# Moving the weights' sums to ScalarE's DMA queue, and a second tile for the last multiplications, in a hybrid encoder layer on one core

## Chip, core and metric

The kernel runs on one core of a Trainium2 chip. The metric is the device time of one execution in microseconds (us); several executions were timed, and one more was taken with the hardware profiler. A core has five engines that matter here: TensorE (PE, matrix products; PEld is its weight load), VectorE (DVE), ScalarE (ACT), GpSimd (POOL) and SyncE (SP, which here only issues DMAs). Each engine works through its own instructions in order; DMAs are issued as instructions of an engine, here of SP, GpSimd or ScalarE, and wait in that engine's order.

## The reference

One layer of an encoder over 512 tokens of width 1024: four parallel token mixers with one input projection, merged by gates; a cross-attention into 256 memory tokens; and a gated feed-forward part. All is float32. The change touches the feed-forward part only:

```
hf  = _rms_norm(x, norm_ffn_pre[l])
u   = _dwconv_causal(hf @ w_up[l], ffn_dw[l]) + ffn_dw_b[l]       # w_up: 1024 x 5632, three taps along the tokens
u_g, u_v = jnp.split(u, 2, axis=-1)
yff = (jax.nn.silu(u_g) * u_v) @ w_down[l]                        # w_down: 2816 x 1024
x   = x + _rms_norm(yff, norm_ffn_post[l])                        # mean square over the 1024 columns, then a weight per column
```

## The kernel before

A float32 product is made of three products of a coarser type: each operand is split into a high part (a cast on ScalarE, L183 or L1384) and the rest, its low part (a subtraction on VectorE, L184 or L1385), and `mm3` (L232) issues high x high, high x low and low x high. Weights come by DMA from SP's queue into tiles `wr` (two of them), are split into tiles `wh` and `wl` (four of each, taken in turn), and are then read by PE. `run_blocks` (L196) splits a block's weights three blocks ahead of its products.

**The up-projection** (`up_jobs`, L1285). 44 blocks n of 128 columns of w_up, gate and value columns in turn, n = 2j + i. After the first four blocks each takes 24 products of 128 x 512 on PE into one PSUM bank; the banks have two tags, `mm` and `av`, in turn, with two banks each. `done` (L1288) empties the bank: ScalarE adds the bias and the last tap (L1292), VectorE the two other taps (L519, called in L1293) into the same tile `c`. After a value block ScalarE takes a tanh (L1296) and VectorE forms silu(gate) x value (L1297, L1299) into the tiles `qa` and `qb`.

**The sums for the down-projection.** The product with w_down is made by a scheme with seven products of 2 x 2 blocks in place of eight (M1 to M7), which needs sums and differences of blocks on both sides. `activation_sums` (L1341) forms those of the activations on GpSimd, four instructions for each of 11 pairs. Those of the weights are formed during the up-projection: `weight_pair(q)` (L1348) loads the pair q of 128 x 1024 blocks of w_down into two tiles `wp` (two pairs fit, as the tag has four buffers), and `weight_sums(q)` (L1353) makes four subtractions or additions in place on VectorE (L1357 to L1360) and stores both tiles to `sums`, a buffer in DRAM (L1362). Before the change the loads and the stores are DMAs of GpSimd's queue. The first two pairs are loaded when block 3 is done; the sums of pair q, its stores and the load of pair q + 2 are placed at block n = 3q + 6, the sums right behind the taps of that block.

**The down-projection** (`down_jobs`, L1364). 22 steps load tiles `dw` from w_down and from `sums` on SP's queue (L1379); `dw` has the same four buffers as `wp`. Phase 0 computes M1, M6, M5 and M7 for all 11 pairs, phase 1 M2, M3 and M4. `middle` (L1446) joins the first four; the last four pairs of phase 1 are held back and done product by product in `ends` (L1490), whose instructions on PE, VectorE, ScalarE and GpSimd keep the order that is written there: M4 for token tiles 0 and 1, then M2 and M3 of tile 0, then M2 and M3 of tile 1. For each, `whole` (L1494) adds the product to a partial sum on VectorE (L1502), `result` (L1469) takes the mean square on ScalarE (`square`, L1439, an activation that also reads out its sum) and multiplies by the post norm's weight on VectorE (L1478); when both halves of a token tile are there, GpSimd makes the reciprocal root (`rstd_of`, L262 and L265), and `finish` (L1481) scales, adds the residual (L1487) and stores (L1488, SP's queue). `finish` of a tile is written after the next product's `result`. The last half is scaled and stored in two pieces.

The lines of the code that order the sums before the change:

```
q = n // 3 - 2
if n % 3 == 0 and q < NF // 2:
    with tc.issue_after(st["last"]):
        weight_sums(q)
    if q + 2 < NF // 2:
        weight_pair(q + 2)
```

Of the kernel before, what the change touches and what calls it, by code (L numbers as in the profile page):

```python
# [16 lines left out]
F32 = mybir.dt.float32  # L17
F32R = mybir.dt.float32r
AF = mybir.ActivationFunctionType
# [5 lines left out]
P = 128  # L25
S = 512
D = 1024
# [6 lines left out]
NF = DFF // P  # L34
EPS = 1e-6
WB = 2 * 520
# [46 lines left out]
def hybrid_layer(ctx: ExitStack, tc: tile.TileContext, a: dict, out: bass.AP):  # L83
    nc = tc.nc
    V, A, G, PE, SP = nc.vector, nc.scalar, nc.gpsimd, nc.tensor, nc.sync


    gp = ctx.enter_context(tc.tile_pool(name="g", bufs=1))
# [7 lines left out]
    def bank(tag=None):  # L96
        if tag is None:
            turn_of.n += 1
            tag = "av" if turn_of.shared and turn_of.n % 2 else "mm"
        return psum.tile([P, 512], F32, tag=tag, name=f"ps_{tag}", bufs=2)  # L100
# [7 lines left out]
    w_up, w_down = a["w_up"][0], a["w_down"][0]  # L108
# [19 lines left out]
    for i in range(8):  # L128
        n = ("wh", "wl")[i % 2]
# [3 lines left out]
        elif i < 6:  # L133
            n = ("fz_raw", "fz", "fe", "fu", "fd")[i - 1]
# [55 lines left out]
    def cols(w, c0, n=P, k0=0, nk=NK):  # L190

        return w[k0 * P:(k0 + nk) * P, c0:c0 + n].rearrange("(k p) c -> p k c", p=P), [P, nk, n]
# [45 lines left out]
    def channel_major(ps, w, act, sl=slice(0, S)):  # L238

        hi, lo = w  # L240
        nk = hi.shape[1]
        for k in range(nk):
            mm3(ps[:, sl], hi[:, k, :], lo[:, k, :], act[0][:, k, sl], act[1][:, k, sl], k == 0, k == nk - 1)
            if k == 3 < nk - 1:
                bg.tick()
# [51 lines left out]
    m1 = tc.tile_pool(name="m1", bufs=1)  # L297
# [62 lines left out]
    for i, plan in enumerate(plans):  # L360
        r_t = m1p.tile([P, P], F32, tag="fbias" if i == 2 else "ck", name=f"rows{i}", bufs=2)
        n = 0
# [116 lines left out]
    def pc(name, j=0, n=1):  # L479
        i, base = where[name]  # L480
        return par[i][:, base + j:base + j + n]
# [33 lines left out]
    def taps(dst, src, w, n):  # L515

        for k in range(n - 1):
            s = n - 1 - k
            ins = V.scalar_tensor_tensor(dst[:, s:], src[:, :S - s], w(k), dst[:, s:], ALU.mult, ALU.add)  # L519
        return ins  # L520
# [486 lines left out]
    ns = SimpleNamespace()  # L1007
# [262 lines left out]
    sums = dram.tile([NF // 2 * P, 2 * D], F32, name="sums")  # L1270
    ns.pair = {}

    def open_ffn():
        bg.drain("n1")
        close(ns.work_)
        close(ns.xp_)
        close(ns.xm_)
        ns.fp_, ns.fp = new_pool("ffn", False)
        ns.work = ns.fp
        ns.quart = [(ns.fp.tile([P, 4, S // 2], F32, tag=f"qa{q}", name="qa"),  # L1280
                     ns.fp.tile([P, 3, S // 2], F32, tag=f"qb{q}", name="qb")) for q in range(NF // 2)]
        ns.post = ns.fp.tile([P, D], F32, name="g_ffn")
        G.dma_start(ns.post, a["norm_ffn_post"][0].partition_broadcast(P))

    def up_jobs():  # L1285
        st, held = {}, []

        def done(j, i, ps):  # L1288
            if i == 0:
                st[j] = ns.fp.tile([P, 2, S], F32, tag="c", name="c", bufs=2)  # L1290
            c, ch = st[j], i * NF + j
            A.activation(c[:, i], ps, AF.Identity, bias=pc("fb", ch), scale=pc("fdw2", ch))  # L1292
            st["last"] = taps(c[:, i], ps, lambda k: pc("fdw01", k * 44 + ch), 3).ins  # L1293
            if i == 1:
                th = ns.fp.tile([P, S], F32, tag="th", name="th")
                A.activation(th, c[:, 0], AF.Tanh, scale=0.5)  # L1296
                V.scalar_tensor_tensor(th, th, 1.0, c[:, 0], ALU.add, ALU.mult)  # L1297
                x = ns.quart[j // 2]
                V.scalar_tensor_tensor(x[j % 2][:, 0:2].rearrange("p a b -> p (a b)"), th, 0.5, c[:, 1],  # L1299
                                       ALU.mult, ALU.mult)  # L1300
                if j % 2:
                    activation_sums(*x)


        for n in range(2 * NF):
            def body(hi, lo, n=n):
                j, i = divmod(n, 2)
                if n > 3:
                    ps = bank()
                    channel_major(ps, (hi, lo), ns.hf)  # L1310
                    done(j, i, ps)
                    q = n // 3 - 2
                    if n % 3 == 0 and q < NF // 2:
                        with tc.issue_after(st["last"]):
                            weight_sums(q)
                        if q + 2 < NF // 2:
                            weight_pair(q + 2)
                    return
                if n == 0:
                    bg.drain("n0")  # L1320
                ps = bank(("mm", "sc")[n % 2])
                (channel_major if n else by_pass)(ps, (hi, lo), ns.hf, slice(0, S // 2))
                held.append((j, i, ps, (hi, lo)))
                if n == 3:
                    open_ffn()
                    for j, i, ps, w in held:
                        (channel_major if i or j else by_pass)(ps, w, ns.hf, slice(S // 2, S))
                        done(j, i, ps)
                    weight_pair(0)
                    weight_pair(1)  # L1330
            yield *cols(w_up, n % 2 * DFF + n // 2 * P), body, V, same, HALF_SHIFT if n < 4 else 0
# [9 lines left out]
    def activation_sums(x, z):  # L1341

        G.tensor_tensor(x[:, 2], x[:, 1], z[:, 1], ALU.add)
        G.tensor_tensor(x[:, 3], x[:, 0], x[:, 1], ALU.subtract)
        G.tensor_tensor(x[:, 1], x[:, 2], x[:, 0], ALU.subtract)
        G.tensor_tensor(z[:, 2], z[:, 0], x[:, 1], ALU.subtract)

    def weight_pair(q):  # L1348
        pair = ns.pair[q] = [ns.fp.tile([P, D], F32, tag="dw", name="wp", bufs=4) for _ in range(2)]
        for i in range(2):  # L1350
            G.dma_start(pair[i], w_down[(2 * q + i) * P:(2 * q + i + 1) * P, :])

    def weight_sums(q):  # L1353

        pair = ns.pair.pop(q)
        (b11, b12), (b21, b22) = ((x[:, :S], x[:, S:]) for x in pair)
        V.tensor_tensor(b22, b22, b12, ALU.subtract)  # L1357
        V.tensor_tensor(b12, b12, b11, ALU.subtract)
        V.tensor_tensor(b11, b22, b11, ALU.add)
        V.tensor_tensor(b21, b21, b11, ALU.subtract)  # L1360
        for i in range(2):
            G.dma_start(sums[q * P:(q + 1) * P, i * D:(i + 1) * D], pair[i])  # L1362

    def down_jobs():  # L1364
        pairs, hold, half = NF // 2, 4, S
# [77 lines left out]
        gains = [slice(i * 512, (i + 1) * 512) for i in range(2)]  # L1443
# [25 lines left out]
        def result(t, i, x, dst, pieces=1):  # L1469

            ms[t, i] = square(x, i, pieces)
            r = None
            if (t, 1 - i) in ms:
                *early, last = ms[t, 1 - i] + ms[t, i]
                if len(early) == 2:
                    G.tensor_tensor(early[0], early[0], early[1], ALU.add)
                r = rstd_of(ns.fp, [early[0], last])
            V.tensor_tensor(dst, x, ns.post[:, gains[i]], ALU.mult)  # L1478
            return r
# [10 lines left out]
        def ends():  # L1490

            m1, u, z7, z = (parts[n] for n in ("m1", "u", "z7", "z"))

            def whole(name, t, x, pieces=1):  # L1494

                for c in range(pieces):
                    cut = slice(c * S // pieces, (c + 1) * S // pieces)
                    for q, job, ws in held:
                        for (n, a), w in zip(work[1, job], ws):
                            if n == name:  # L1500
                                step(name, t, q, a, w, 1, cut)
                    V.tensor_tensor(x[:, cut], x[:, cut], banks[name][t][:, cut], ALU.add)  # L1502
                return x

            waiting = None
            with tc.manual_schedule(engines={e.engine for e in (PE, V, A, G)}):
                for name, t, i, x in (("M4", 0, 0, z7), ("M4", 1, 0, z7), ("M2", 0, 0, m1), ("M3", 0, 1, u),
                                      ("M2", 1, 0, m1), ("M3", 1, 1, u)):
                    token = t + 2 * (name == "M4")
                    x = whole(name, t, x[:, t])  # L1510
                    r = result(token, i, x, x)
                    if waiting:
                        finish(*waiting)
                        waiting = None
                    if r is not None:
                        waiting = token, {1: z[:, t], 0: x} if name == "M4" else {0: m1[:, t], 1: x}, r
                finish(*waiting)

        def body(phase, q, job, ws):
# [67 lines left out]
```

## Time and profile before

| | us |
|---|---|
| median of 3 runs (lowest to highest) | 1073.1 (1071.56 to 1074.53) |
| profiled execution | 1070.76 |
| its span, first to last instruction | 1069.0 |
| PE busy in the span | 1056.0 |
| DVE / ACT / POOL busy in the span | 764.4 / 489.2 / 171.1 |
| mean granted TensorE clock | 0.996 |

In a row of a timeline stand the start and the length in us, the engine, the line, the operation, what it writes and reads (names of tiles, with the buffer numbers left out) with shapes, how many instructions are merged (x), and in brackets how long the engine had been idle and what released it. POOLq, ACTq and SPq are the issuing of DMAs and the like; such instructions are not counted as busy. Ends of products on PE are modelled. The up-projection's steady part runs from about 735 to 942 us of the span and the down-projection from there; the last product ends near 1057.6 us.

### The profile page before, as it was taken

To read this page: it belongs to the slowest core of one execution; us is meant where nothing else is said; L and a number is where in the kernel's file an instruction comes from. 1 tells how busy PE (TensorE), PEld (TensorE's weight loads), DVE (VectorE), ACT (ScalarE), POOL (GpSimd) and SP (SyncE) were. 2 spreads that over 40 slices of the span, in tenths; PEclk is the share of its full clock that TensorE was granted. 3 is DMA by queue.
4 is the path that set the end of the run, shared out by engine and by line. 5 is a ranking of instruction groups with operands and counts; after the bars stand their busy time and mean duration, and the time that the engine had idled before them with its cause. 6 is when DMAs were issued, how large, how long until landed. Compare 5 with 4: busy or idle time off the path is not lost.

```text
span 1069.0 us, 14449 instructions
## 1 busy us (share of the span) xinstructions
PE 1056.0 (99%) x5387; PEld 898.2 (84%) x5387; DVE 764.4 (72%) x1211; ACT 489.2 (46%) x809; POOL 171.1 (16%) x277
## 2 busy tenths in 40 slices
PE   9999999999999999999999999999999999999995
PEld 8888888888888988888888899998888888888884
DVE  7899996467666367766464386787778888777795
ACT  5322222466564365555453364554333333446661
POOL 4000001000101024323000030031223332111002
PEclk9999999999999999999999999999999999999998
DMA  6433333332222243332354443235576766626652
GB/s 212 112 98 90 93 100 98 99 90 75 74 80 81 59 126 95 97 99 81 97 158 149 146 139 99 80 87 190 177 246 217 225 221 219 211 79 205 210 186 79
DMA packets 158524, 141.04 MB, mean 132 GB/s; under 512 B 5056, under 2 KB 134701, under 8 KB 158454
## 3 DMA queue, kind: packets, MB, share of 16 engines
q1 hardware_dynamic: 149555, 108.50, 33.8%
q0 software_dynamic: 8896, 31.61, 8.7%
q8 instruction: 42, 0.69, 0.3%
q14 instruction: 29, 0.23, 0.1%
q10 hardware_dynamic: 2, 0.00, 0.0%
HBM read 126.45 MB, written 13.65 MB: 131 GB/s over the span
## 4 chain that ended last, share of the span: by engine, by line
PE 98%; DVE 1%; ACT 0%; issue 0%; POOL 0%; POOLq 0%; DVEq 0%; ACTq 0%
PE ps_mm L225 52%; PE ps_av L225 30%; PE ps_sc L225 8%; PE ps_tr L229 3%; PE ps_tr L225 2%; PE ps_mm L432 1%; PE ps_av L432 1%; PE ps_mm L374 0%; ACT junk L1439 0%; DVE o L1487 0%; PE ps_sc L379 0%; DVE wr L1487 0%; DVE wr L1478 0%; DVE z L1487 0%; DVE o L1502 0%; DVE wr L1502 0%
## 5 line engine op out<-in xcount | busy, mean ns | idle before, releaser
L183 ACT CAST wh<-wr 128x1024 fp32r<-128x1024 f32 (+1 forms) x150 | 157.0, 1050 | 291.6 <-PE ps_mm L225 183.9
L184 DVE TENSOR_TENSOR wl<-wr,wh 128x1024 fp32r<-128x1024 f32 (+1 forms) x150 | 189.2, 1263 | 113.1 <-ACT wh L183 112.7
L225 PE MATMUL ps_mm<-hth,wh 128*128 128x512 f32 (+1 forms) x616 | 231.4, 382 | 0.3 <-ACT hth L152 0.2
L225 PE MATMUL ps_mm<-hth,wl 128*128 128x512 f32 (+1 forms) x616 | 230.0, 380 | 0.0
L225 PE MATMUL ps_mm<-htl,wh 128*128 128x512 f32 (+1 forms) x616 | 229.9, 380 | 0.0
L225 PEld LDWEIGHTS ps_mm<-hth,wh 128*128 128x128 f32 x616 | 114.3, 188 | 21.2 <-ACT hth L152 0.5
L225 PEld LDWEIGHTS ps_mm<-hth,wl 128*128 128x128 f32 x616 | 114.0, 188 | 21.0
L225 PEld LDWEIGHTS ps_mm<-htl,wh 128*128 128x128 f32 x616 | 114.0, 188 | 20.5 <-DVE htl L153 0.2
L225 PE MATMUL ps_av<-hth,wh 128*128 128x512 f32 (+1 forms) x328 | 122.4, 373 | 0.0
L225 PE MATMUL ps_av<-htl,wh 128*128 128x512 f32 (+1 forms) x328 | 122.4, 373 | 0.0
L225 PE MATMUL ps_av<-hth,wl 128*128 128x512 f32 (+1 forms) x328 | 122.3, 373 | 0.0
L586 DVE SCALAR_TENSOR_TENSOR y<-y,par,y 128x499 f32<-128x499 f32 (+28 forms) x120 | 82.4, 731 | 0.2
L225 PEld LDWEIGHTS ps_av<-htl,wh 128*128 128x128 f32 x328 | 61.7, 188 | 10.9
L225 PEld LDWEIGHTS ps_av<-hth,wh 128*128 128x128 f32 x328 | 61.6, 188 | 10.9
L225 PEld LDWEIGHTS ps_av<-hth,wl 128*128 128x128 f32 x328 | 61.5, 188 | 10.8
L225 PE MATMUL ps_mm<-y,wh 128*128 128x512 f32 x192 | 61.2, 394 | 0.0
L1385 DVE TENSOR_TENSOR wl<-dw,wh 128x1024 fp32r<-128x1024 f32 x32 | 40.2, 1261 | 12.3 <-ACT wh L1384 12.2
L1384 ACT CAST wh<-dw 128x1024 fp32r<-128x1024 f32 x32 | 33.4, 1051 | 23.0 <-PE ps_tr L225 8.4
L225 PEld LDWEIGHTS ps_mm<-y,wh 128*128 128x128 f32 x192 | 35.4, 188 | 6.8
L909 POOL TENSOR_SCALAR fbias<-ck,cq 128x128 f32<-128x128 f32 (+3 forms) x32 | 27.5, 865 | 68.1 <-DVE st L915 63.9
L225 PE MATMUL ps_mm<-y,wl 128*128 128x512 f32 x96 | 37.6, 392 | 0.0
L1296 ACT ACTIVATE th<-c 128x512 f32<-128x512 f32 x22 | 13.9, 632 | 49.4 <-DVE c L519 49.4
(436 smaller groups left out, 2026.4 us busy)
## 6 DMA issues: line engine op xcount, KB each, us to landing
wr<-in_w_up SPq DMA_DIRECT2D x44, 512.0 KB
wr<-in_w_in SPq DMA_DIRECT2D x38, 512.0 KB
wr<-in_w_gate SPq DMA_DIRECT2D x32, 512.0 KB
wp<-in_w_down POOLq DMA_DIRECT2D x22, 512.0 KB, 5.5
sums<-wp POOLq DMA_DIRECT2D x22, 512.0 KB, 4.2
dw<-sums SPq DMA_DIRECT2D x44, 256.0 KB
wr<-in_w_branch SPq DMA_DIRECT2D x16, 512.0 KB
dw<-in_w_down SPq DMA_DIRECT2D x11, 512.0 KB
```

Of the source, the lines that this page charges most:

```text
L183: order(A.copy(hi, raw[:, :n]))
L184: low.tensor_tensor(lo, raw[:, :n], hi.bitcast(F32), ALU.subtract)
L225: PE.matmul(ps, lhs, rhs, start=start, stop=stop)
L229: PE.transpose(ps, x, ident[:n, :n])
L432: keep(PE.matmul(banks[c][:, :S // 2], w[p == 1][:, k, c * P:(c + 1) * P], ht[p == 2][:, i * 4 + k, :S // 2], start=(i, p, k) == (0, 0, 0) ...
L586: V.scalar_tensor_tensor(dst[:, s:], src[:, :S - s], pc("conv_dw", k * 4 + j), dst[:, s:], ALU.mult, ALU.add)
L909: G.tensor_scalar(bias[:, :w], ck[j][:, :w], -1.0, cq[:, qt, head:head + 1], ALU.mult, ALU.add)
L1296: A.activation(th, c[:, 0], AF.Tanh, scale=0.5)
L1384: A.copy(hi, x)
L1385: V.tensor_tensor(lo, x, hi.bitcast(F32), ALU.subtract)
```

## The change

Part one splits the storing from the sums and moves loads and stores of the pairs to ScalarE's queue. The four sums stay at block n = 3q + 6 behind its taps; the two stores are placed at the next block behind its bias activation (L1292), and the load of pair q + 2 one block later, again behind that activation. Part two gives the multiplications by the post norm's weight in `ends` a destination of their own: two tiles of the tag `dw` and one of the tag `wr`, which are free by then. The sum that the square reads is no longer overwritten; `finish` reads the new tiles.

```diff
-            A.activation(c[:, i], ps, AF.Identity, bias=pc("fb", ch), scale=pc("fdw2", ch))
-            st["last"] = taps(c[:, i], ps, lambda k: pc("fdw01", k * 44 + ch), 3).ins
+            st["first"] = A.activation(c[:, i], ps, AF.Identity, bias=pc("fb", ch), scale=pc("fdw2", ch)).ins
+            st["taps"] = taps(c[:, i], ps, lambda k: pc("fdw01", k * 44 + ch), 3).ins
...
                     q = n // 3 - 2
-                    if n % 3 == 0 and q < NF // 2:
-                        with tc.issue_after(st["last"]):
-                            weight_sums(q)
-                        if q + 2 < NF // 2:
-                            weight_pair(q + 2)
+                    if 0 <= q < NF // 2:
+                        with tc.issue_after(st["taps" if n % 3 == 0 else "first"]):
+                            (weight_sums, store_sums, weight_pair)[n % 3](q + 2 * (n % 3 == 2))
                     return
...
     def weight_pair(q):
+        if q >= NF // 2:
+            return
         pair = ns.pair[q] = [ns.fp.tile([P, D], F32, tag="dw", name="wp", bufs=4) for _ in range(2)]
         for i in range(2):
-            G.dma_start(pair[i], w_down[(2 * q + i) * P:(2 * q + i + 1) * P, :])
+            A.dma_start(pair[i], w_down[(2 * q + i) * P:(2 * q + i + 1) * P, :])

     def weight_sums(q):
-        pair = ns.pair.pop(q)
+        pair = ns.pair[q]
...
+    def store_sums(q):
+        pair = ns.pair.pop(q)
         for i in range(2):
-            G.dma_start(sums[q * P:(q + 1) * P, i * D:(i + 1) * D], pair[i])
+            A.dma_start(sums[q * P:(q + 1) * P, i * D:(i + 1) * D], pair[i])
...
+            spare = [ns.fp.tile([P, D], F32, tag="dw", name="o", bufs=4) for _ in range(2)]
+            spare.append(gp.tile([P, WB], F32, tag="wr", name="wr", bufs=2)[:, :D])
...
                     token = t + 2 * (name == "M4")
-                    x = whole(name, t, x[:, t])
-                    r = result(token, i, x, x)
+                    c = t if name == "M4" else i
+                    o = spare[2 if name == "M4" else t][:, gains[c]]
+                    r = result(token, i, whole(name, t, x[:, t]), o)
...
                     if r is not None:
-                        waiting = token, {1: z[:, t], 0: x} if name == "M4" else {0: m1[:, t], 1: x}, r
+                        other = z[:, t] if name == "M4" else spare[t][:, gains[0]]
+                        waiting = token, {1 - i: other, i: o}, r
```

## The prediction

> **What bounds the kernel now.** I read the page's busy times and chain first, then busy time by stage, then the timelines of one stretch of the FFN and of the end.
>
> ```profile
> span 1069.0 us, 14449 instructions
> PE 1056.0 (99%) x5387; PEld 898.2 (84%) x5387; DVE 764.4 (72%) x1211; ACT 489.2 (46%) x809; POOL 171.1 (16%) x277
> ...
> PE 98%; DVE 1%; ACT 0%; issue 0%; POOL 0%; POOLq 0%; DVEq 0%; ACTq 0%
> ```
> ```profile
> 735.55:941.80 206.25, 206.25 (x912) 170.76 (x911) 163.58 (x201) 78.92 (x98) 59.35 (x80) 1.00 0.65 207
> 941.80:1040.00 98.20, 98.20 (x434) 81.16 (x433) 77.67 (x82) 61.62 (x74) 3.82 (x4) 1.00 0.57 180
> 1040.00:1057.70 17.70, 17.63 (x78) 14.26 (x76) 10.48 (x17) 3.73 (x11) 4.34 (x6) 1.00 0.15 59
> 1057.70:1069.00 11.30, 0.00 (x0) 0.00 (x0) 4.56 (x8) 0.72 (x2) 1.35 (x2) 0.60 0.26 94
> ```
>
> Columns of the second view: stretch, length, busy time of PE, PEld, DVE, ACT, POOL, PE clock, DMA share, GB/s. From 735.55 to 1040 us, which holds the up-projection (where the loads and stores of the weights' sums run) and most of the down-projection, PE has no gap. There, work on another engine is worth nothing unless it makes PE wait. Only the last 11.3 us have no PE work; they are a chain of VectorE, ScalarE, GpSimd and a store.
>
> **Part 1: 44 DMAs move from GpSimd's queue to ScalarE's.** The instruction order of the changed kernel, as built, has PE's instructions in the same sequence as before. So the question is only whether PE ever finds its weights or a PSUM bank late.
>
> ```profile
> 838.48 5.44 PE ps_av L225 x24
> ...
> 860.24 5.44 PE ps_av L225 x24
> ```
> ```profile
> 843.73 1.05 ACT L183 CAST wh<-wr 128x1024 fp32r<-128x1024 f32 x1 [0.27 <-PE ps_av L225]
> 844.68 0.77 ACT L1292 ACTIVATE c<-ps_av,par 128x512 f32<-128x512 f32 x1
> ...
> 860.04 1.05 ACT L183 CAST wh<-wr 128x1024 fp32r<-128x1024 f32 x1 [3.71 <-PE ps_mm L225]
> ```
> ```profile
> 844.81 1.22 DVE L184 TENSOR_TENSOR wl<-wr,wh 128x1024 fp32r<-128x1024 f32 x1 [0.63 <-ACT wh L183]
> 845.96 1.53 DVE L519 SCALAR_TENSOR_TENSOR c<-ps_av,par,c 128x510 f32<-128x510 f32 x2
> ...
> 856.83 0.69 DVE L1360 TENSOR_TENSOR wp<-wp 128x512 f32<-128x512 f32 x1
> ```
>
> *The cover.* The cast at 843.73 waits for the block that began at 838.48 to free its weight tile. There are four such tiles, so PE next reads this one at 860.24 (838.48 + 4 x 5.44). Its low part is ready at 844.81 + 1.22 = 846.03: 14.2 us early. The bank of that block is emptied by 845.96 + 1.53 = 847.49 and written again at 860.24, as two tags with two banks alternate: 12.7 us early. ScalarE has to be late by more than 12 us before PE sees it.
>
> ```profile
> 857.82 0.54 POOL L1362 DMA_DIRECT2D sums<-wp  x1 [1.23 <-DVE wp L1360]
> ...
> 864.11 0.57 POOL L1351 DMA_DIRECT2D wp<-in_w_down  x1 [1.16 <-DMA sums<-wp]
> ```
> ```profile
> 0.72 0.52 ACTq L319 DMA_DIRECT2D gain_src<-in_norm_mix_pre  x1
> ```
> ```profile
> 728.10 1.05 ACT L183 CAST wh<-wr 128x1024 fp32r<-128x1024 f32 x1 [3.74 <-PE ps_mm L225]
> ```
>
> *What is added on ScalarE.* The one DMA that ScalarE issues today takes 0.52 us. 40 of the 44 fall in the up-projection after 735.55: 20.8 us beside 78.9 busy of 206.25. Two waits come with them. A second store waits for the last subtraction of its pair, which ends at 856.83 + 0.69 = 857.52; with its issue ScalarE is free at about 858.1, and its next cast waits for PE until 860.04 anyway. A second load waits for the store a block earlier to land; GpSimd issued it at 864.11, 6.3 us after the store. Behind it stands a tanh or a cast, and behind the tanh VectorE's next steps; a hold of 1 to 2 us is well inside 12. The first four loads stand ahead of the cast at 728.10, which sat 3.74 us waiting for PE: 4 x 0.52 = 2.1 us fit there. SP's queue gets its first four loads for the down-projection in one run ahead of a load of the up weights: under a microsecond inside the same cover.
>
> ```profile
> POOL wp L1351 <- DMA sums<-wp: 28.4, 15, 3.3
> ```
>
> On GpSimd these waits (28.4 us in all, 15 times) leave the way of the activations' sums (L1343 to L1346), which the down-projection reads only later: no gain. I take nothing for all this; without the cover it would be about 1 us for each of 11 pairs, 11 us.
>
> *The transfers.*
>
> ```profile
> q1 hardware_dynamic: 149555, 108.50, 33.8%
> q0 software_dynamic: 8896, 31.61, 8.7%
> ```
> ```profile
> wp<-in_w_down POOLq DMA_DIRECT2D x22, 512.0 KB, 5.5
> sums<-wp POOLq DMA_DIRECT2D x22, 512.0 KB, 4.2
> ```
>
> 44 x 0.524 = 23.1 MB change queue. By the shares of the 1069 us, the software queue costs 93.0 us / 31.61 MB = 2.94 us for a MB, the hardware one 361.3 / 108.50 = 3.33. As an estimate the move costs 23.1 x 0.39 = 9 us of DMA time, spread over 206 us: the share goes from 0.65 to 0.69. With rows of 4 KB on either queue it may also fall. Neither end reaches PE.
>
> **Part 2: the end.** Before, each multiplication by the post norm's weight (L1478) overwrites what ScalarE squares (L1439), so it waits for the square. Now it writes another tile and follows the addition (L1502) directly.
>
> ```profile
> 1045.90 0.84 PE L225 MATMUL ps_mm<-n,a 128*128 128x512 f32 x3
> ...
> 1054.07 0.84 PE L225 MATMUL ps_sc<-dwr,a 128*128 128x512 f32 x3
> ...
> 1056.79 0.84 PE L225 MATMUL ps_tr<-dwr,a 128*128 128x512 f32 x3
> ```
> ```profile
> 1046.79 0.69 DVE L1502 TENSOR_TENSOR z<-z,ps_mm 128x512 f32<-128x512 f32 x1 [0.55 <-PE ps_mm L225]
> ...
> 1057.40 0.69 DVE L1478 TENSOR_TENSOR wr<-wr,g_ffn 128x512 f32<-128x512 f32 x1 [0.85 <-ACT junk L1439]
> ...
> 1059.34 0.68 DVE L1502 TENSOR_TENSOR o<-o,ps_tr 128x512 f32<-128x512 f32 x1
> 1060.87 0.69 DVE L1478 TENSOR_TENSOR o<-o,g_ffn 128x512 f32<-128x512 f32 x1 [0.85 <-ACT junk L1439]
> 1062.40 0.75 DVE L1487 SCALAR_TENSOR_TENSOR wr<-wr,st_r,res 128x512 f32<-128x512 f32 x1 [0.84 <-POOL st_r L265]
> ```
> ```profile
> 853.11 0.68 DVE L1357 TENSOR_TENSOR wp<-wp 128x512 f32<-128x512 f32 x1
> 853.82 0.69 DVE L1358 TENSOR_TENSOR wp<-wp 128x512 f32<-128x512 f32 x1
> ```
>
> PE ends its last product at 1056.79 + 0.84 = 1057.63, and the last addition starts only at 1059.34: VectorE is late, because each multiplication stood 0.85 us behind a square. An addition can start 0.05 us after PE (1045.90 + 0.84 = 1046.74, start 1046.79). Now the last two rounds without these waits. PE has the last but one product at 1054.91; addition at 1054.96; multiplication 0.71 later (the spacing of two steps on the same tiles at 853.11 and 853.82) at 1055.67; from there to the next addition VectorE needs 1059.34 - 1057.40 = 1.94, so it is free at 1057.61. The last addition starts at 1057.68, set by PE: **1.66 us** earlier.
>
> ```profile
> 1060.65 0.19 ACT L1439 ACTIVATION_READ_ACCUMULATOR junk<-o 128x1 f32 x1
> ```
> ```profile
> 1060.93 0.79 POOL L262 TENSOR_SCALAR st_m<-pm,pm 128x1 f32<-128x1 f32 x1 [4.17 <-ACT junk L1439]
> 1061.81 0.56 POOL L265 TENSOR_TENSOR st_r<-st_m,nhalf 128x1 f32<-128x1 f32 x1
> ```
> ```profile
> 706.89 0.30 POOL L262 TENSOR_SCALAR st_m<-pm,pm 128x1 f32<-128x1 f32 x1 [4.57 <-ACT junk L1084]
> ```
> ```profile
> 706.82 0.69 DVE L1085 TENSOR_TENSOR o<-ps_av,g_post 128x512 f32<-128x512 f32 x1 [0.19 <-ACT junk L1084]
> ```
>
> A second gain follows on GpSimd. Its step st_m took 0.79 us at 1060.93, while VectorE multiplied two SBUF tiles (1060.87 to 1061.56), and ended 0.16 after that; the same step took 0.30 beside a multiplication that reads PSUM (706.82). Now the multiplication runs from 1058.39 to 1059.08 and the square's sum is there at 1060.84 - 1.66 = 1059.18, so st_m finds VectorE idle: 0.79 - 0.30 = **0.49** less, and st_r and the last scaling follow at once. Between nothing and 0.49 I take 0.49, as the row fits the overlap to the end. The Trainium skill, page "SBUF — State Buffer", section "Who interferes with whom", has the rule: a VectorE instruction with two SBUF inputs and a GpSimd instruction that reads SBUF block each other for the whole instruction. The trace agrees (0.79 against 0.30); without the rule the sum would stop at 1.66.
>
> The rest of the end (two pieces, the stores) moves along unchanged. Sum: -1.66 - 0.49 = -2.15 us. The span becomes 1066.9, the profiled execution 1070.76 - 2.15 = 1068.6. It ran 2.34 us below the median of the runs shown, 1073.1; the same shift there gives **1070.9 us**, 0.2% faster. A difference under 0.3%, 3.2 us, is about what a measurement of this kernel can't tell from none.
>
> **Rivals.**
> *Slower: the transfers become the bound of the up-projection.* If moved to the hardware queue beside SP's loads they cost so much DMA time that the 0.65 share exceeds 1, PE waits for weights. It decides at 0.35 x 206 = 72 us more for 23.1 MB, so at 2.94 + 3.1 = 6.1 us for a MB, twice either row; against it. At a share of 1.1 it costs 0.1 x 206 = 21 us: 1092.
> *Nothing reaches the end.* The change doesn't do what it says: the multiplication still waits, or the last store sets the end. Against it: the end follows from the last scaling in the chain. Time 1073.1.
> *More gained than the profile shows.* The median is 2.34 us over the profiled execution. If that is PE waiting for slow transfers of GpSimd's queue in other executions, it goes too: 1073.1 - 2.15 - 2.34 = 1068.6. For it: only that the difference exists; against it: 12 us of cover. The Trainium skill, the same page and section, says that a DMA which VectorE seems to stall is one whose descriptors GpSimd writes, and that a DMA from ScalarE's queue is free of this; no run here shows it.
>
> **How the numbers follow.** Forecast 0.70, more gained 0.14, nothing 0.08, slower 0.08. The three runs of before lie 1.5 us to either side of their median. With that spread, of the forecast 0.17 falls below 1069.9 (over 0.3% faster) and the rest within; of "more" 0.13 below. Faster 0.30. Slower: 0.08 and 0.02 of "nothing": 0.10. Same 0.60. The range 1068.4 to 1073.4 takes in "more", both ends of 1.66 to 2.15 and "nothing", and leaves out the slower rival and the outer spread. The forecast's own range is 1069.4 to 1072.6.
>
> **What would show it.** In the profile after: no PE gap from 735 to 1057; ScalarE's issues near 0.5 us, with holds under 2 us; the multiplications start 0.7 us after their additions; the last addition 0.05 us after PE's end; the last st_m near 0.30; span about 2.1 us shorter. A gap of PE in the up-projection, or a span shorter by over 3 us, would prove the steps wrong.

## The result, and the profile after

| | before | after |
|---|---|---|
| median of 7 runs each, us (lowest to highest) | 1071.93 (1071.39 to 1074.53) | 1067.17 (1066.48 to 1070.44) |
| profiled execution, us | 1070.76 | 1067.17 |
| its span, us | 1069.0 | 1065.4 |

After stands to before as 0.9956, with a 95% interval of 0.9942 to 0.9969: 4.8 us less, where 2.15 were forecast, and a time below the range. The page of after, first its busy times and its two DMA queues:

```profile
span 1065.4 us, 14430 instructions
PE 1056.1 (99%) x5387; PEld 897.8 (84%) x5387; DVE 763.7 (72%) x1211; ACT 488.1 (46%) x809; POOL 147.4 (14%) x233
...
q1 hardware_dynamic: 149555, 108.50, 34.1%
q10 hardware_dynamic: 6338, 23.08, 5.8%
q0 software_dynamic: 2560, 8.54, 2.8%
```

Busy time by stage in after, cut where the prediction cut it (length; busy PE, PEld, DVE, ACT, POOL; clock, DMA share, GB/s):

```profile
735.55:941.80 206.25, 206.25 (x912) 170.79 (x912) 161.86 (x201) 79.46 (x98) 38.14 (x40) 1.00 0.64 207
941.80:1040.00 98.20, 98.20 (x434) 81.18 (x433) 77.79 (x82) 61.20 (x75) 3.82 (x4) 1.00 0.58 182
```

PE again has no gap over the whole up-projection and most of the down-projection, and is busy for the same 1056 us. The 23.08 MB now stand on q10, ScalarE's queue, and cost 5.8% of 16 engines' span. The gain is behind PE's last product. The end of after (VectorE, ScalarE, GpSimd and SP merged in order of time; a dotted line where rows are left out):

```profile
1055.63 0.69 DVE L1506 TENSOR_TENSOR wr<-wr,ps_sc 128x512 f32<-128x512 f32 x1 [1.30 <-PE ps_sc L225]
1056.35 0.69 DVE L1482 TENSOR_TENSOR o<-wr,g_ffn 128x512 f32<-128x512 f32 x1
...
1058.35 0.69 DVE L1506 TENSOR_TENSOR o<-o,ps_tr 128x512 f32<-128x512 f32 x1
1059.07 0.69 DVE L1482 TENSOR_TENSOR o<-o,g_ffn 128x512 f32<-128x512 f32 x1
...
1059.95 0.30 POOL L262 TENSOR_SCALAR st_m<-pm,pm 128x1 f32<-128x1 f32 x1 [4.49 <-ACT junk L1443]
1060.34 0.56 POOL L265 TENSOR_TENSOR st_r<-st_m,nhalf 128x1 f32<-128x1 f32 x1
1060.93 1.54 DVE L1491 SCALAR_TENSOR_TENSOR o<-o,st_r,res 128x512 f32<-128x512 f32 x3 [1.17 <-POOL st_r L265]
```

Each multiplication (L1482, which was L1478) now follows its addition after 0.72 us. PE's last product ends at 1058.31 by the trace, 0.68 later than before. Compared product by product, 0.46 of it is there by 100 us (PE has gaps of 0.36 and 0.16 us near 8 us, which before had not) and the rest arises between 327 and 419 us, all of it ahead of the steps that the change touches. From there the last scaling needs 1060.93 - 1058.31 = 2.62 us, against 1062.40 - 1057.63 = 4.77: **2.15 us less, as worked out**. But from the last scaling to the end of the span it is 4.44 us instead of 6.56 (the span ends at 1065.37, before at 1068.96). That is another **2.12 us**, in the part that was to "move along unchanged". The two spans thus differ by 2.15 + 2.12 - 0.68 = 3.59 us.

What lies there is seen in the instructions of the line that opens the program's context (L1583 before, L1591 after): the closing instructions of all engines carry it. Among them are DRAINs, instructions on no tile that each engine has behind its last work, and waits by which the engines meet before the program ends (the closing meeting). The columns are engine, operation, count, then least, median and largest duration in ns, and first and last start. First before, then after:

```profile
L1583 POOLq DRAIN  x3: 40/102/6409, 1061.8 to 1068.7; - x3
L1583 SPq DRAIN  x3: 7/7/7, 1066.6 to 1068.4; - x3
```
```profile
L1591 POOLq DRAIN  x3: 40/102/2814, 1060.3 to 1065.1; - x3
L1591 SPq DRAIN  x3: 7/7/7, 1064.5 to 1064.8; - x3
```

GpSimd closes with a DRAIN that starts when st_r does. Before, it starts at 1061.77 and lasts 6.41 us, to 1068.18, and the closing meeting of all engines, 0.78 us ahead of the span's end, waits for it. SP has finished its waits for the last stores at 1066.70, 1.48 us sooner. After, the same instruction lasts 2.81 us and ends at 1063.11, and SP, at 1064.60, is the later one. GpSimd issues 70 DMAs before and 26 after (counted in the trace): (6.409 - 2.814) / 44 = 0.082 us for each. The rest of the 2.12 us is SP's, which finishes 4.30 us behind the last scaling's start before, and 3.67 after. 1.48 + 0.63 = 2.11.

### The profile page after: what moved, and what is told of

It is laid out like the page before. It is cut to its first block, busy times and chain, and to the rows that moved or that the text cites. A ratio compares the mean times of both kernels' runs of the same rounds, so it can differ in the third digit from the quotient of the medians.

```text
span 1065.4 us, 14430 instructions
## 1 busy us (share of the span) xinstructions
PE 1056.1 (99%) x5387; PEld 897.8 (84%) x5387; DVE 763.7 (72%) x1211; ACT 488.1 (46%) x809; POOL 147.4 (14%) x233
## 3 DMA queue, kind: packets, MB, share of 16 engines
q10 hardware_dynamic: 6338, 23.08, 5.8%
## 4 chain that ended last, share of the span: by engine, by line
PE 98%; DVE 1%; DMA 0%; POOL 0%; ACT 0%; issue 0%; POOLq 0%; DVEq 0%; ACTq 0%
PE ps_mm L225 53%; PE ps_av L225 30%; PE ps_sc L225 8%; PE ps_tr L229 3%; PE ps_tr L225 3%; PE ps_mm L432 1%; PE ps_av L432 1%; DMA xs<-in_x 0%; DVE o L1491 0%; POOL st_r L265 0%; PE ps_av L416 0%; POOL st_m L262 0%; DVE nt L411 0%; DVE wr L1506 0%; DVE o L1482 0%
```

## The experiments

**The theory:** two gains of equal size that hardly touch. The second tile gives 2.15 us; the shorter queue of GpSimd gives 2.1 us, by its closing DRAIN, which is paid for each DMA that GpSimd issued, and by SP's closing waits. **Rivals:** the whole gain is the second tile's; GpSimd's transfers had been slowing PE; the DRAIN counts bytes, or instructions. The first four have 12 runs each beside 35 of the kernel before (median 1071.72 us, 1070.66 to 1075.67). The others have one execution each, so they are read by their traces and not by their times.

### Only the queue

After without its part two.

```diff
-            spare = [ns.fp.tile([P, D], F32, tag="dw", name="o", bufs=4) for _ in range(2)]
-            spare.append(gp.tile([P, WB], F32, tag="wr", name="wr", bufs=2)[:, :D])
...
-                    r = result(token, i, whole(name, t, x[:, t]), o)
+                    x = whole(name, t, x[:, t])
+                    r = result(token, i, x, x)
```

> Only the DMAs move to ScalarE's queue; the multiplications at the end still overwrite what the square reads. Theory (GpSimd's closing DRAIN lasts about 0.08 us for each DMA that GpSimd has issued, and with 70 of them it ends later than SP's wait for the last stores): the last scaling comes as in before, the DRAIN falls from 6.4 to about 2.8 us, SP's wait sets the end; 1.5 to 2.1 us faster than before. Rival (the queue plays no part at the end, all of the gain is from the tiles): no difference. Rival (GpSimd's transfers make PE wait in the up-projection in most executions): over 2 us faster with the end as in before.

1069.34 us (12 runs), ratio 0.9977 [0.9964, 0.9990]. Its end, first the timeline's three steps on VectorE and GpSimd, then the closing instructions:

```profile
1061.08 0.69 DVE L1482 TENSOR_TENSOR o<-o,g_ffn 128x512 f32<-128x512 f32 x1 [0.85 <-ACT junk L1443]
1061.14 0.80 POOL L262 TENSOR_SCALAR st_m<-pm,pm 128x1 f32<-128x1 f32 x1 [4.16 <-ACT junk L1443]
...
1062.62 0.75 DVE L1491 SCALAR_TENSOR_TENSOR wr<-wr,st_r,res 128x512 f32<-128x512 f32 x1 [0.85 <-POOL st_r L265]
```
```profile
L1587 POOLq DRAIN  x3: 40/93/2816, 1062.0 to 1066.8; - x3
```

The wait of 0.85 us behind the square and the st_m of 0.80 are there as before; from PE's end (1057.84) to the last scaling it takes 4.78 us, as before. But the span ends 4.49 behind the scaling. The queue alone gives 2.1 us there, and from 735.55 to 1056 us PE has no gap, as in before. The median is 2.4 us below that of before, a little over the 1.5 to 2.1 expected.

### Only the tiles

Before with part two: the two blocks of the diff that name `spare`, and nothing else.

> Only the new tiles at the end; the DMAs stay on GpSimd's queue. Theory: the last scaling stands 2.6 us behind PE's end instead of 4.8, the DRAIN stays at 6.4 us and still sets the end, 6.5 us from last scaling to the end of the span as in before; 2.15 us faster than before. Rival (the shorter way from the last scaling to the end comes with the tiles): 4.3 us faster, DRAIN or not.

1069.40 us (12 runs), ratio 0.9980 [0.9968, 0.9992].

```profile
1060.43 0.30 POOL L262 TENSOR_SCALAR st_m<-pm,pm 128x1 f32<-128x1 f32 x1 [4.49 <-ACT junk L1439]
1060.81 0.56 POOL L265 TENSOR_TENSOR st_r<-st_m,nhalf 128x1 f32<-128x1 f32 x1
1061.41 1.54 DVE L1487 SCALAR_TENSOR_TENSOR o<-o,st_r,res 128x512 f32<-128x512 f32 x3 [1.17 <-POOL st_r L265]
```
```profile
L1587 POOLq DRAIN  x3: 40/93/6411, 1060.8 to 1067.7; - x3
```

PE's end (1058.79) to the scaling: 2.62 us. Scaling to the span's end: 6.55, with a DRAIN of 6.41. This is the forecast of 2.15 us, alone. By the traces the halves add up: 2.07 and 2.15 us behind PE's end, against 4.27 for both. The medians (2.4 and 2.3 us, against 4.1 for both, below) agree with that within their intervals, of 1.3 to 1.6 us to either side.

### Before, with GpSimd's queue drained early

```diff
-        G.tensor_tensor(z[:, 2], z[:, 0], x[:, 1], ALU.subtract)
+        ns.last = G.tensor_tensor(z[:, 2], z[:, 0], x[:, 1], ALU.subtract).ins
...
+            with tc.issue_after(ns.last):
+                G.drain()
```

The added DRAIN (L1493) stands behind the last of the activations' sums, some 100 us ahead of the end, where GpSimd is idle. All 70 DMAs stay on GpSimd's queue.

> The kernel before with one DRAIN more on GpSimd, behind its last sum of activations, some 95 us ahead of the end. Theory (a DRAIN works off what GpSimd's DMAs have left, and only once): the early one lasts about 5.8 us where GpSimd is idle, the closing one under 1 us, SP sets the end; 1.5 to 2.1 us faster than before, with all 70 DMAs still on GpSimd's queue. Rival (the closing DRAIN waits for the fetch of GpSimd's last instructions): the closing one stays near 6.4 us, no difference. Rival (it is a fixed cost of having used the queue): no difference.

1069.86 us (12 runs), ratio 0.9985 [0.9972, 0.9999].

```profile
L1493 POOLq DRAIN  x1: 6586/6586/6586, 968.6 to 968.6; - x1
```
```profile
L1585 POOLq DRAIN  x3: 34/93/667, 1065.4 to 1070.8; - x3
L1585 SPq DRAIN  x3: 7/7/7, 1070.3 to 1070.6; - x3
```

The long DRAIN has moved forward to 968.6, where it hides under PE. It lasts 6.59 us, longer than the 5.8 expected; the last of the activations' sums, of 0.74 us, runs inside it, as st_r does in the closing one. The closing one takes 0.67 us, and the span ends 5.05 us behind the scaling instead of 6.56. The 1.5 us are thus GpSimd's DRAIN and neither transfers nor ScalarE's queue. 0.6 us of after's gain at this place are missing: SP's part.

### After, again

> The changed kernel on the same chip as the three others, for comparison. Theory: 3.7 to 4.8 us faster than before; the DRAIN 2.8 us, 4.4 us from the last scaling to the end of the span.

1067.61 us (12 runs), ratio 0.9958 [0.9944, 0.9973]; 2.62 us from PE's end to the scaling, 4.44 to the end, a DRAIN of 2.817 us. All three numbers of after are repeated.

### What the DRAIN counts

Four variants of after. **Half**: the stores in `store_sums` back on GpSimd's queue. **Tiny**: 44 more DMAs of GpSimd, of 8 elements each. **Operations**: 44 more instructions of GpSimd that are no DMAs. **Drained**: the added DRAIN of the third experiment.

```diff
# half, in store_sums
-            A.dma_start(sums[q * P:(q + 1) * P, i * D:(i + 1) * D], pair[i])
+            G.dma_start(sums[q * P:(q + 1) * P, i * D:(i + 1) * D], pair[i])
# tiny, in store_sums, for i in range(4)
+            G.dma_start(ns.tiny[0:1, (4 * q + i) * 8:(4 * q + i) * 8 + 8], w_down[0:1, (4 * q + i) * 8:(4 * q + i) * 8 + 8])
# operations, in store_sums, for i in range(4)
+            G.memset(ns.tiny[:, (4 * q + i) * 8:(4 * q + i) * 8 + 8], 0.0)
```

> The kernel after with its 22 stores of the weights' sums back on GpSimd's queue and the 22 loads left on ScalarE's: GpSimd issues 48 DMAs, between the 26 of after and the 70 of before. Theory (GpSimd's closing DRAIN costs a fixed 0.69 us and 0.0817 us for each DMA that GpSimd issued, from 6.409 us at 70 and 2.814 at 26): 0.69 + 48 x 0.0817 = 4.6 us. It starts 0.63 us ahead of the last scaling, so it ends 4.0 us behind it, about where SP's closing waits end too; the span ends 4.4 to 5.0 us behind the last scaling, against 4.44 after and 6.56 before. Rival (not the number of DMAs but whether the stores or the loads are there at all): the DRAIN is near 2.8 or near 6.4 us. No gap of PE in the up-projection by either.

> The kernel after with 44 more DMAs of GpSimd, four at each of the 11 places where a pair's stores are issued, each of 8 elements (32 bytes) from one row of w_down into a tile that nothing reads: GpSimd again issues 70 DMAs, but moves next to no bytes more. Theory (the closing DRAIN is paid per DMA that GpSimd issued, whatever its size): the DRAIN takes about 6.4 us and the span ends about 6.5 us behind the last scaling, as before the change. Rival (it is paid per descriptor or per byte, of which the 44 large DMAs had many): the DRAIN stays near 2.8 us and the span ends 4.4 us behind the last scaling.

> The kernel after with 44 more small instructions on GpSimd that are no DMAs (each sets 128 x 8 elements of a tile that nothing reads to zero), at the same 11 places: 26 DMAs of GpSimd. Theory (only DMAs that GpSimd issued count): the closing DRAIN stays at 2.8 us and the span ends 4.4 us behind the last scaling. Rival (the DRAIN grows with the number of instructions that GpSimd had to work through): it rises toward 6.4 us and the span ends later.

> The kernel after with one more DRAIN on GpSimd, behind the last of the activations' sums, some 90 us ahead of the end. Theory (the end is the later of GpSimd's closing DRAIN and SP's closing waits for the last stores): the early DRAIN takes about 2.8 us, the closing one falls to about 0.67 us, and the span still ends 4.4 us behind the last scaling, since SP has been the later of the two since the change. Rival (GpSimd's DRAIN itself sets the end in every case): the end comes 2.1 us sooner, 2.3 us behind the last scaling.

The closing instructions of half, tiny, operations and drained, in this order:

```profile
L1591 POOLq DRAIN  x3: 40/102/4612, 1062.7 to 1068.2; - x3
L1591 SPq DRAIN  x3: 7/7/7, 1067.7 to 1068.0; - x3
```
```profile
L1597 POOLq DRAIN  x3: 46/106/6406, 1060.4 to 1067.3; - x3
L1597 SPq DRAIN  x3: 7/7/7, 1064.7 to 1067.1; - x3
```
```profile
L1594 POOLq DRAIN  x3: 40/102/2816, 1059.7 to 1064.5; - x3
```
```profile
L1593 POOLq DRAIN  x3: 34/102/669, 1060.0 to 1064.8; - x3
L1593 SPq DRAIN  x3: 7/7/7, 1064.2 to 1064.5; - x3
```

| | GpSimd's DMAs | closing DRAIN, us | last scaling to span's end, us | profiled execution, us |
|---|---|---|---|---|
| before | 70 | 6.41 | 6.56 | 1070.76 |
| half | 48 | 4.61 | 5.19 | 1070.27 |
| after | 26 | 2.81 | 4.44 | 1067.17 |
| tiny | 70 | 6.41 | 6.56 | 1069.40 |
| operations | 26 | 2.82 | 4.44 | 1066.53 |
| drained | 26, 0 since the early DRAIN | 0.67 | 4.43 | 1066.87 |

The DRAIN of half is the 4.6 us that were worked out. 44 DMAs of 32 bytes cost the same as 44 of 512 KB, and 44 other instructions cost nothing: it counts DMAs, not bytes and not work. In both variants the added instructions wait for nothing that the stores wait for, so GpSimd ran them ahead of the places named (the DMAs from 720.9 to 757 us, the others from 720.2 to 722); the DMAs cost as much at the end as those of before, issued up to 923 us. In tiny SP has finished at 1064.74 and the meeting still waits for GpSimd until 1066.8. In drained the early DRAIN takes 2.99 us (2.8 expected), the closing one gets 2.1 us shorter and the end doesn't move: SP's waits set it now. The end is the later of the two. Half ended later than expected, 5.19 against at most 5.0: its DRAIN ends 3.98 us behind the scaling's start, but SP finishes only 4.43 behind it.

### SP's part

By the trace, SP closes with waits on eight semaphores (counters that a DMA raises when it lands) in a fixed row (100, 102, 103, 105, 106, 107, 109, 110), which the DMAs of SP's and ScalarE's queues take in turn. The last store has 103 before, 109 after, 100 in half. Two variants of after add one and four DMAs of 8 elements on ScalarE's queue, which shifts the turn.

```diff
# in store_sums, with k = 1 or 4
+        if q < k:
+            A.dma_start(ns.tiny[0:1, q * 8:q * 8 + 8], w_down[0:1, q * 8:q * 8 + 8])
```

> The kernel after with four more DMAs on ScalarE's queue, one at the store of each of the first four pairs, each of 8 elements into a tile that nothing reads. GpSimd's 26 DMAs and its closing DRAIN (2.8 us) stay. The DMAs of SP's and ScalarE's queues take eight semaphores in turn (100, 102, 103, 105, 106, 107, 109, 110), and SP's closing waits go through them in that order; the last store has 103 before and 109 after, as 44 more DMAs are four steps round. Theory (where the last store's semaphore stands in the row of waits decides how many waits are left behind its landing): four more DMAs bring it back to 103, SP ends its waits 4.3 us behind the start of the last scaling instead of 3.7, and the span ends 5.0 to 5.1 us behind it. Rival (the difference of 0.6 us comes from the shorter queue of GpSimd or from the second tile): 4.44 as after.

> The kernel after with one more DMA of 8 elements on ScalarE's queue, at the store of the first pair. Theory (the last store's place in SP's closing waits decides): its semaphore goes from 109 to 110, the last of the row, so one wait fewer (0.06 to 0.07 us) is left behind its landing and the span ends about 4.37 us behind the start of the last scaling. Rival (the place does not matter): 4.44.

| | last store's semaphore | last scaling to SP's finish, us | from the passed wait for the last store to SP's finish, us | last scaling to span's end, us |
|---|---|---|---|---|
| before | 103 | 4.30 | 0.78 | 6.56 |
| after | 109 | 3.67 | 0.20 | 4.44 |
| four more | 103 | 4.04 | 0.47 | 4.81 |
| one more | 110 | 3.61 | 0.13 | 4.38 |

One more came out as expected (4.37). Four more brought the semaphore back to 103, but only 0.37 of the 0.63 us (5.0 to 5.1 us to the span's end expected, 4.81 measured). Each wait left behind the landing costs 0.06 to 0.08 us. The row also has a pause of 0.36 to 0.38 us that no landing explains, in all twelve traces: from the wait on 105 to that on 106 in the four kernels that store the sums from GpSimd's queue (before: 1065.99 to 1066.36), and from 102 to 103 in the other eight. So in before it stands behind the last store's wait, in after ahead of it, and with four more just ahead of it (1064.05 to 1064.41; the store landed at 1064.30), and behind that wait the row runs without it (1064.41 to 1064.88). The place in the row is thus shown to move the end, by one trace of each variant; what makes the pause, and why it changes its place, stays open. One more DMA saves 0.06 us over after, too little for the times to show (one execution, 1067.72).

## Why the prediction was right and wrong

**Part 1 at no cost for PE: right.** PE's gapless 206.25 us in the quoted row show it. The issues on ScalarE were cheaper than the 0.52 us taken, and the holds lay inside the cover:

```profile
757.37 1.05 ACT L183 CAST wh<-wr 128x1024 fp32r<-128x1024 f32 x1 [0.96 <-PE ps_av L225]
758.25 0.34 ACTq L1366 DMA_DIRECT2D sums<-wp  x1
758.33 0.77 ACT L1292 ACTIVATE c<-ps_av,par 128x512 f32<-128x512 f32 x1
760.31 0.33 ACTq L1366 DMA_DIRECT2D sums<-wp  x1
762.81 1.05 ACT L183 CAST wh<-wr 128x1024 fp32r<-128x1024 f32 x1 [3.71 <-PE ps_mm L225]
763.04 0.34 ACTq L1352 DMA_DIRECT2D wp<-in_w_down  x1
```

The second store leaves 2.06 us behind the first, and the cast that follows still waits for PE until 762.81. The DMA share of the stage went to 0.64 instead of 0.69, from 0.65: on ScalarE's queue these 23.08 MB cost 5.8% of 1065.4 us, 2.68 us for a MB, below both rates from which the 9 us of extra DMA time were estimated. Those rates were means over unlike transfers. GpSimd's queue lost 23.07 MB and went from 93.0 us (8.7%) to 29.8 (2.8% of 1065.4): the same transfers had cost 2.74 us for a MB there, so the move itself costs no more DMA time. The slower rival (1092) falls with it.

**The last addition, 1.66 us: right.** It starts at 1058.35, 0.04 behind PE's end at 1058.31. **The st_m, 0.49 us: right.** 0.30 us instead of 0.79, in after and in the kernel with the tiles alone; 0.80 where the multiplication stands beside it. The Trainium skill, page "SBUF — State Buffer", section "Who interferes with whom", has a GpSimd read and a VectorE instruction with two SBUF inputs shut each other out; these four traces agree with it. Together the two terms came to 2.15 us, and 2.15 was measured.

**The step that failed: "The rest of the end (two pieces, the stores) moves along unchanged."** It got 2.12 us shorter. The prediction followed the work of the end up to the stores and took what comes behind, 6.56 us from the last scaling, for a constant. Part 1 was checked only against PE; GpSimd's DMAs had a price at the end that is paid wherever in the program they were issued. The prediction itself named a span shorter by over 3 us as a sign of a wrong step; it is 3.6 us shorter. The profile before had it: the DRAIN of 6.41 us in the closing line, and SP done 1.5 us before it ended. The chain of waits didn't tell it, as it goes back from the last scaling and gives GpSimd's sequencer a share of 0%.

**The base.** The forecast was put on a median of 1073.1 from three runs; with seven it is 1071.93. Of the 3.73 us between 1070.9 and 1067.17, that is 1.17, and the closing 2.12; the other 0.44 is within the spread of the runs.

**The rival "more gained than the profile shows"** gave 1068.6, the nearest number, but by another mechanism: PE waiting for GpSimd's transfers of the sums. No trace has such a wait in the up-projection, so that it came nearest is chance. Executions of one kernel do differ by 4 to 5 us, and two profiled ones show a cause for a part of it, far from the change. In the kernel with the early DRAIN and in half (here the former), PE waits 1.91 and 1.50 us for a row vector that GpSimd's queue loads in an earlier stage:

```profile
396.81 0.37 POOL L909 TENSOR_SCALAR fbias<-ck,cq 128x128 f32<-128x128 f32 x1 [3.99 <-DMA ck<-crows]
397.26 0.29 POOL L911 TENSOR_SCALAR_AFFINE_SELECT fbias<-fbias 128x128 f32<-128x128 f32 x1
397.59 0.29 DVE L915 CUSTOM_DVE_ANT_0 e<-ps_sc,fbias 128x128 f32<-128x128 f32 x1 [5.11 <-POOL fbias L911]
...
397.94 0.50 PE L225 MATMUL ps_sc<-qk 128*128 128x256 f32 x2 [1.91 <-DVE st L915]
```

In the profiled execution of before that wait is 2.61 us and PE has no gap. This DMA is on the same queue in both kernels, so the change doesn't remove it. That all the longer executions have this gap wasn't seen, since a timed run leaves no trace.

## What to carry to other kernels

Look behind the last store: list the closing instructions of every engine and see which one the end waits for, since a cost can be laid up anywhere in the program and paid only there. A DMA moved off GpSimd's queue saves 0.08 us at the end for as long as GpSimd's closing DRAIN is the later side; a DRAIN of GpSimd placed under other work (1.5 us here) saves that without moving anything, and neither gives more once SP's waits for the last stores are later. And an engine's cover in the steady part says nothing of the end, so each part of a change is priced in both places.

## What the runs showed of the hardware that was not expected

- **GpSimd's DRAIN costs about 0.082 us for each DMA that GpSimd issued since the DRAIN before it:** 6.41 us for 70, 4.61 for 48, 2.81 for 26, and 0.67 after an early DRAIN, in all cases with st_r's 0.56 us inside. Sizes of 32 bytes and 512 KB cost the same. All these DMAs had landed long before, the last at 929 us in before and at 759 us in tiny, and idle time doesn't work the cost off: in after GpSimd stands idle for 79.87 us up to 1046.30. The Trainium skill, page "VectorE: DVE Perf Modes", section "The DRAIN you can't avoid", gives the DRAINs that the runtime puts ahead of and behind a kernel as about 12 ns, constant, on all five engines. Those here carry a line of the kernel, so the page need not mean them: SP's (7 ns) and ScalarE's last (14 ns) are as short, but GpSimd's first closing one isn't, and it varies with the program.
- **The place of the last store's semaphore in SP's closing waits moves the end** by 0.06 to 0.08 us a step, and by more where a pause of 0.36 to 0.38 us falls behind it.
- **An issue of a 512 KB DMA on ScalarE's queue takes 0.33 to 0.35 us** in 41 of after's 44 (0.36 and twice 0.45 in the others), against 0.54 to 0.56 on average for the same DMAs on GpSimd's; a MB of them cost 2.68 us of DMA time on ScalarE's queue and 2.74 on GpSimd's.
